# Two-part probabilities and values in a DSA attention tail, with engine orders written out as tables

## The chip, the cores and the metric

One core of a Trainium2 chip runs the kernel. Its engines are TensorE (PE in the rows, with its weight loads as PEld), VectorE (DVE), ScalarE (ACT), GpSimd (POOL) and SyncE (SP), which issues the loads. The metric is device time in microseconds for one call; lower is better.

## The reference

Two layers over x of 512 tokens and 1024 channels, each a mixer and a SwiGLU FFN (d_ff 2816), with a root-mean-square norm ahead of each.

The even layer's mixer has two halves. DSA attention: 8 query heads and 2 key/value heads of 64; an index score with 4 small heads picks for each query the best 128 keys; the softmax runs over these.

```
rel = relu(einsum(qi, k_idx)); score = einsum(rel, w) * IDX_SCALE   # causal
_, sel = lax.top_k(score, n_sel)                                    # n_sel = 128
p = softmax(q . k_sel * 64**-0.5);  o = p @ v_sel
```

A pooling half takes moving averages over 2, 4, 8 and 16 tokens, a 128x128 product for each group, and a scale. Both halves together go through `ev_w_out` (1024x1024).

The odd layer's mixer is stick-breaking attention with 16 heads of 64: `a = exp(log_sigmoid(z) - reversed cumsum of softplus(z))`, `o = a @ v`, then `od_w_out`. Each FFN is `(silu(h@w1) * (h@w3)) @ w2`.

## The kernel before

Activations are held transposed: channels on the partitions, the 512 tokens along a row, so x is eight tiles of 128x512 (`xs`). A weight or activation that needs more than one fp32r product is held as a rounded part and a rest, (h, l), and a dense product is three fp32r products: wh·ah, wh·al, wl·ah (`prods`, L202; lines L205 to L207). 

Each layer's attention is a list of small steps, `EVEN_ORDER` and `ODD_ORDER`. Every step is a function that issues its instructions; the program is traced in that order, and a scheduler with a model of the durations then decides the order on each engine, under the data dependences. Each engine runs its own list strictly in order, and waits for the others by semaphores. PSUM has eight banks of 128x512; `take` and `give` hand them out, and `EVEN_BANKS` (L47) says which step takes which banks.

Even layer, in the names of the steps: `qi`, `ki` are projections of the index heads, `st` and `sb` the norm's statistics and their broadcast, `q`, `kj` the projections of queries and keys, `z` the index scores (L750, L751, then ACT L753, DVE L757/L759, POOL L760), `sel` the choice of keys in blocks of 128 queries (MAX8 L770, MATCH_REPLACE8 L771, 16 rounds in a block, and the mask `bias[b]` at L773), `nat` (`step_nat`) makes v, 128 tokens on the partitions, in one tile for each key/value head j with zeros in the other head's half (L794). Then, for block b, head pair j and chunk k of 128 keys: `s` (`step_s`) computes four score tiles with the mask added as a third product (L874 to L876), takes a row maximum (DVE L879, POOL L880), the exponential (ACT L882), its reciprocal (DVE L888) and scales (L889: L177 on ACT or L181 on POOL). `pt` (`step_pt`) transposes four heads' probabilities into one of two 't' banks (L896), ACT copies them out (L898). `av` (`step_av`) multiplies them by v in F32 (`Bank.mm`, recorded at L225) into one bank 'o' for both j, 2(b+1) products, and at the last ACT writes oh (L911) and DVE ol (L912). Blocks 0 and 1 end before the last masks are there; blocks 2 and 3 are the last. `u`, `y`, `op` are the pooling half and its output products, `oa` the attention's output products; at each `oa` (and at each output step `x` of the odd layer) a chunk of x is complete, and `Norm.chunk` makes its parts hh and hl (L268, L269) and adds its squares on POOL into acc (L280).

The FFN begins with the first products of tiles that need no norm factor (`Plain`, `start`), with `nrm.stats()` behind 24 of them (PE L286, DVE L288, POOL L291); later tiles (`Job`) use sums of weights and of pairs of chunks (POOL L352 to L355 and L492 to L495). `bcast` (L293) spreads the factor over the partitions (PE L297); `follow` ties each of its products behind a product of the first Job.

Of the kernel before, what the change touches and what calls it, by code (L numbers as in the profile page):

```python
# [8 lines left out]
F32 = mybir.dt.float32  # L9
F32R = mybir.dt.float32r  # L10
# [6 lines left out]
P = 128  # L17
# [5 lines left out]
EPS = 1e-6  # L23
NSEL = 128

SPLIT = {'k1': ('pool', 'dve'),
 'ki': ('act', 'dve'),
 'nat_0': ('dve', 'dve'),
# [15 lines left out]
SPHI = {'A': 'act', 'B': 'pool', 'C': 'act'}  # L44
AHI = {'A': 'pool', 'B': 'act', 'C': 'act'}
KDUP = 'pool'
EVEN_BANKS = {'mm': (0, 1, 2), 's': (3, 4), 't': (5, 6), 'o': (7,), 'oa': (0, 1, 2, 3, 4, 5, 6, 7)}  # L47
ODD_BANKS = {'qk': (0,), 'A': (1,), 'B': (3,), 'C': (5,), 'o': (6,), 'v': (1, 2, 5, 6, 7), 'x': (0, 3, 4, 5), 'st': (4, 6), 'y': (7, 3, 4, 2, 1, 5, 0, 6)}
PRN = ('act', 'pool', 'act', 'pool')
WRAW = 3  # L50
# [54 lines left out]
]  # L105
NEG = -1e30
GONE = -3e38
GONE_TEST = -2.5e38
# [3 lines left out]
def f32(ap):  # L112
    return ap.bitcast(F32)
# [3 lines left out]
def tile_trunk(ctx, tc, x, gains, qk_gain, pool_scale, w_a, w_nat, pool_w, w_o0, w_qk, w_v, w_o1, w13, w2, out):  # L117
# [91 lines left out]
    def follow(m, first, why):  # L209

        tc.add_manual_dep(
            m.ins,
            first.ins.name,
            mybir.DependencyInfo(mybir.DependencyClass.NoSync, mybir.DependencyReason.DATA),
            reason=why,
        )
# [24 lines left out]
    class Norm:  # L241
# [48 lines left out]
            self.rcol = stat.tile([P, NB], F32, name=f"rcol{i}", tag="rcol")  # L290
            gp.tensor_tensor(self.rcol, ms, mhalf[:, 0:NB], op=ALU.pow)  # L291

        def bcast(self, banks=range(8), after=None):  # L293
            i = self.idx
            pb = take(banks)
            for b in range(NB):
                m = te.matmul(  # L297
                    pb[:, b * P : (b + 1) * P],
                    self.rcol[:, b : b + 1].to_broadcast([P, P]),
                    ident,  # L300
                    start=True,
                    stop=True,
                )
                if after is not None:
                    follow(m, after, "behind products that wait for less")
            self.rb = stat.tile([P, T], F32, name=f"rb{i}", tag="rb")
            ve.tensor_copy(self.rb, pb)
            give(pb)
# [93 lines left out]
    def ffn(stage):  # L402
# [220 lines left out]
        for f in range(1, NP):  # L623
            for w in range(2):
                x = Job(f, w)
                for who, p in ((x, 1), (x, 2), (y, 4), (x, 6), (y, 3), (x, 5), (x, 7)):
                    if who is not None:
                        m = who.prod(p)
                    elif p == 4:
                        nrm.bcast(after=m)  # L630
                        for d in start:
                            d.done()
                y = x
                q, r = divmod(f, 2)
                if q:
                    Down(q - 1, 2 * r + w)
# [13 lines left out]
    def even(nrm, nxt, w_first, after):  # L650
        with ExitStack() as es_wk:
# [22 lines left out]
            vs = [ap.tile([P, NB, P], F32, name=f"v{j}") for j in range(2)]  # L674
            for j in range(2):
                gp.memset(vs[j][:, :, OWN[1 - j]], 0.0)
            bias = {b: ap.tile([P, (b + 1) * P], BF16, name=f"bias{b}") for b in range(NB)}
            gp.memset(bias[0], 0.0)
            gp.affine_select(
# [96 lines left out]
            def step_nat():  # L776
# [14 lines left out]
                for b in range(NB):  # L791
                    ps = pns[b]
                    for j in range(2):
                        ac.activation(  # L794
                            vs[j][:, b, OWN[j]], ps[:, 64 * j : 64 * j + 64], AF.Copy, scale=nrm.rcol[:, b : b + 1]
                        )
                    for j in range(2):
                        ksq = wk.tile([P, 64], F32, name=f"ksq{b}_{j}", tag="ksq")
                        ac.activation(
                            ksq, ps[:, 128 + 64 * j : 192 + 64 * j], AF.Square, accum_out=kss[:, b, j : j + 1]  # L800
                        )
                    ac.copy(kn[:, b].rearrange("p a b -> p (a b)"), ps[:, 128:256])
                    give(ps)
# [89 lines left out]
            def step_pt(b, j, k):  # L893
                pt = take(EVEN_BANKS["t"])
                for c in range(4):
                    te.transpose(pt[:, c * P : (c + 1) * P], S["pr", b, j, c][:, k * P : (k + 1) * P], ident)  # L896
                pT = wk.tile([P, T], F32, name=f"pT{b}_{j}_{k}", tag="pT")
                ac.copy(pT, pt)  # L898
                give(pt)
                S["pT", b, j, k] = pT  # L900

            def step_av(b, j, k):
                if ("po", b) not in S:
                    S["po", b], S["bank", b], S["left", b] = take(EVEN_BANKS["o"]), Bank(), 2 * (b + 1)
                po = S["po", b]
                S["left", b] -= 1
                S["bank", b].mm(po, vs[j][:, k, :], S["pT", b, j, k], stop=(S["left", b] == 0))
                if S["left", b] == 0:
                    bs = slice(b * P, (b + 1) * P)
                    p3 = po.rearrange("p (a b) -> p a b", b=P)  # L910
                    ac.copy(oh[:, :, bs], p3)  # L911
                    ve.tensor_sub(ol[:, :, bs], p3, f32(oh[:, :, bs]))  # L912
                    give(po)
# [330 lines left out]
    ffns[1].run()  # L1244


# [1 line left out]
def _station(w):  # L1248

# [53 lines left out]
```

## Time and profile before

| | before |
|---|---|
| median of 3 runs | 1184.28 us (1182.9 to 1185.0) |
| the profiled execution | 1183.68 us |
| its span in the profile | 1181.9 us |
| PE busy | 1143.6 us (97%) |
| DVE busy | 862.1 us (73%) |
| ACT busy | 606.1 us (51%) |
| POOL busy | 547.9 us (46%) |

The span is what the profile covers, the rest of the 1183.68 lies around it. Busy time is the time that the engine's instructions cover; matmuls are pipelined, so a matmul's duration in a row is longer than the distance to the next. The granted clock is a share of TensorE's full 2.4 GHz; 0.5 is 1.2 GHz. "idle before <-releaser" says how long the engine stood still before an instruction and what ended it.

### The profile page before, as it was taken

The numbers are of one execution on the slowest core, as the hardware profiler recorded it, in microseconds if no ns is written. First come the engines' busy times: TensorE is split into PE (matmuls) and PEld (weight loads), VectorE is DVE, ScalarE is ACT, GpSimd is POOL, SyncE is SP. The second block draws the span as 40 slices with busy tenths as digits, with TensorE's granted clock in tenths as the row PEclk, the third lists the DMA queues.
The fourth block names the chain that finished last, engine by engine and source line by source line (L and its number), as shares of the span: only waits on it lengthen the run. The fifth ranks groups of instructions, "written<-read, shape, count | busy, mean of one in ns | idle before, by whom it ended". The sixth has DMA issues, their size and how long they took to land.

```text
span 1181.9 us, 17814 instructions
## 1 busy us (share of the span) xinstructions
PE 1143.6 (97%) x6854; PEld 1005.8 (85%) x6856; DVE 862.1 (73%) x1180; ACT 606.1 (51%) x929; POOL 547.9 (46%) x506
## 2 busy tenths in 40 slices
PE   7998989999999999999999999999799999999998
PEld 4885747799999999998888888888699999999997
DVE  7699936688778677757467778877678877676764
ACT  5354566454444444436257788866354444444441
POOL 4166646766444444403033345434876444454420
PEclk9999999899999999999999999999999999999999
DMA  5221112123333333323321111114122332333321
GB/s 202 74 87 59 54 36 95 48 90 108 108 107 93 102 105 94 108 73 97 106 94 45 52 36 54 54 54 127 34 90 87 111 109 96 100 108 108 108 90 71
DMA packets 37667, 102.60 MB, mean 87 GB/s; under 512 B 4560, under 2 KB 7120, under 8 KB 37584
## 3 DMA queue, kind: packets, MB, share of 16 engines
q1 hardware_dynamic: 37152, 101.47, 27.5%
q8 instruction: 53, 0.87, 0.3%
q14 instruction: 30, 0.25, 0.1%
q10 hardware_dynamic: 432, 0.02, 0.0%
HBM read 99.37 MB, written 2.10 MB: 86 GB/s over the span
## 4 chain that ended last, share of the span: by engine, by line
PE 73%; DVE 9%; POOL 8%; issue 5%; ACT 3%; DMA 1%; SPq 0%; POOLq 0%; DVEq 0%; ACTq 0%
PE psum L526 10%; PE psum L528 10%; PE psum L527 10%; PE psum L205 10%; PE psum L206 10%; PE psum L207 10%; PE psum L225 6%; DVE score L771 1%; DVE m L770 1%; PE psum L1027 1%; PE psum L1028 1%; PE psum L1029 1%; POOL acc L280 1%; POOL s L494 1%; POOL s L492 1%
## 5 line engine op out<-in xcount | busy, mean ns | idle before, releaser
L599 DVE TENSOR_TENSOR x<-x,psum 128x512 f32<-128x512 f32 x88 | 60.4, 686 | 119.6 <-PE psum L207 119.4
L492 POOL TENSOR_TENSOR s<-raw_w 128x512 f32<-128x512 f32 x40 | 60.2, 1505 | 178.8 <-DMA raw_w<-in_w_dram 154.1
L206 PE MATMUL psum<-gsl,wh_w 128*128 128x512 f32 x352 | 137.7, 391 | 0.0
L207 PE MATMUL psum<-gsh,wl_w 128*128 128x512 f32 x352 | 135.4, 390 | 0.0
L205 PE MATMUL psum<-gsh,wh_w 128*128 128x512 f32 x352 | 135.2, 391 | 0.0
L577 POOL TENSOR_TENSOR c<-c,rb 128x512 f32<-128x512 f32 x40 | 61.2, 1530 | 118.3 <-ACT c L576 118.3
L410 ACT CAST wh_w<-raw_w 128x1024 fp32r<-128x1024 f32 (+1 forms) x48 | 47.0, 980 | 114.5 <-PE psum L206 106.6
L526 PE MATMUL psum<-hh,wh_t 128*128 128x256 f32 x320 | 90.1, 282 | 0.5 <-DVE c L559 0.5
L526 PE MATMUL psum<-hh,wh_a 128*128 128x256 f32 x320 | 90.1, 282 | 0.5 <-ACT wh_a L410 0.5
L528 PE MATMUL psum<-hh,wl_s 128*128 128x256 f32 x320 | 90.3, 283 | 0.0
L526 PE MATMUL psum<-hh,wh_s 128*128 128x256 f32 x320 | 90.3, 283 | 0.0
L527 PE MATMUL psum<-hl,wh_t 128*128 128x256 f32 x320 | 90.3, 282 | 0.0
L527 PE MATMUL psum<-hl,wh_s 128*128 128x256 f32 x320 | 89.9, 281 | 0.0
L527 PE MATMUL psum<-hl,wh_a 128*128 128x256 f32 x320 | 89.8, 281 | 0.0
L528 PE MATMUL psum<-hh,wl_t 128*128 128x256 f32 x320 | 89.7, 280 | 0.0
L528 PE MATMUL psum<-hh,wl_a 128*128 128x256 f32 x320 | 89.6, 281 | 0.0
L410 ACT CAST wh_a<-raw_w 128x1024 fp32r<-128x1024 f32 x40 | 42.0, 1050 | 71.8 <-PE psum L206 57.4
L207 PEld LDWEIGHTS psum<-gsh,wl_w 128*128 128x128 f32 x352 | 66.2, 188 | 12.9
L206 PEld LDWEIGHTS psum<-gsl,wh_w 128*128 128x128 f32 x352 | 66.2, 188 | 12.1
L205 PEld LDWEIGHTS psum<-gsh,wh_w 128*128 128x128 f32 x352 | 65.8, 188 | 11.8
L411 DVE TENSOR_TENSOR wl_a<-raw_w,wh_a 128x1024 fp32r<-128x1024 f32 x40 | 65.8, 1646 | 12.9 <-ACT wh_a L410 12.9
L411 DVE TENSOR_TENSOR wl_w<-raw_w,wh_w 128x1024 fp32r<-128x1024 f32 (+1 forms) x48 | 64.6, 1346 | 3.6 <-ACT wh_w L410 3.5
(357 smaller groups left out, 3780.7 us busy)
## 6 DMA issues: line engine op xcount, KB each, us to landing
raw_w<-in_w_dram SPq DMA_DIRECT2D x88, 512.0 KB, 3.6
raw_w<-in_w_dram SPq DMA_DIRECT2D x80, 256.0 KB, 3.0
raw_v<-in_w_v_dram SPq DMA_DIRECT2D x8, 512.0 KB, 3.7
raw_q<-in_w_qk_dram SPq DMA_DIRECT2D x8, 512.0 KB, 3.6
raw_k<-in_w_qk_dram SPq DMA_DIRECT2D x8, 512.0 KB, 3.7
raw_o<-in_w_o_dram SPq DMA_DIRECT2D x8, 512.0 KB, 3.6
x<-in_x_dram SPq DMA_DIRECT2D x8, 256.0 KB, 4.7
raw_q<-in_w_a_dram SPq DMA_DIRECT2D x4, 512.0 KB, 4.8
```

The lines of the kernel that those rows point to most:

```text
L205: te.matmul(ps, wh, ah, start=(first and i == 0), stop=False)
L206: te.matmul(ps, wh, al, start=False, stop=False)
L207: te.matmul(ps, wl, ah, start=False, stop=(last and i == n - 1))
L225: m = te.matmul(dst, lhsT, rhs, start=self.first is None, stop=stop, skip_group_check=True)
L410: ac.copy(h[:, :n], src)
L411: ve.tensor_sub(l[:, :n], src, f32(h[:, :n]))
L492: gp.tensor_add(z[0], a21, a22)
L526: te.matmul(ps, wh, ah, start=first, stop=False, skip_group_check=True)
L527: te.matmul(ps, wh, al, start=False, stop=False, skip_group_check=True)
L528: m = te.matmul(ps, wl, ah, start=False, stop=(k == KC // 2 - 1), skip_group_check=True)
L577: gp.tensor_mul(d, d, nrm.rb)
L599: ve.tensor_add(xs[n], xs[n], self.ps[i])
```

## The change

- v gets a second pair of tiles, `vp[j]`: in head j's own half the rounded v, in the other half the rest v − rounded v. Eight small copies on ACT and eight subtractions on DVE in `step_nat`.
- In blocks 2 and 3 (`PACKED = 2`) the transposed probabilities are held as h (ACT, rounded) and l (DVE, the rest, out of PSUM); the 't' bank is given back behind both. `packed_av` multiplies `vp[j]` by h and by l, two fp32r products; the half of the bank on the other head's partitions holds the products with v's rest. Each j has a bank of its own, from banks 7 and 2, and ends with a copy of that half (cr, ACT), an add (DVE), and oh (ACT) and ol (DVE) for its 64 partitions.
- `bcast` no longer ties its products behind a Job's.
- `ENGINE_ORDER`: for each engine a list of its instructions' numbers in program order; at the end of the program each one listed is tied, without a semaphore, behind the one listed before it. PE's list has 3212 of its instructions (the whole even layer to the first Jobs of the first FFN, and the last products of that FFN over the odd layer into the last FFN), DVE's 690, ACT's 574, POOL's 355, SP's 110 loads. The rest of both FFNs isn't listed.

Decoded into steps, the lists say among other things: on PE `st` stands within `qi`, `sb` right behind `ki`, `z 1` behind 12 products of `q` (before: 48 of `q 0` and `q 1`); the products of `op` 3 to 7 lie between the scores of block 2 and those of block 3; behind the first score product of block 3 stand 24 score products, 48 transposes and 27 products with v, and then `oa`, in the order 4, 5, 1, 3, 2 for the products with oh, the rest behind; the FFN's statistics stand behind 96 products of oa, 70 of Plain and 22 of Job. On DVE the subtractions for l stand behind the last mask; ahead of it are the eight for v and two reductions of block 2 more than before. On POOL the first pair sum is that of chunks 0 and 1. In the odd layer single products of `q`, `k`, `v` and `x` alternate with the small ones of `z`, `s`, `o`; in the last FFN the statistics stand behind 78 Plain and the factor's broadcast further behind, with 24 Job products between, and POOL's power (L291) ahead of sums of weights. The loads on SP change places: pool_w 2 and 3 earlier, the first of oa ahead of pool_w 1.

```diff
+PACKED = 2
-EVEN_BANKS = {'mm': (0, 1, 2), 's': (3, 4), 't': (5, 6), 'o': (7,), 'oa': (0, 1, 2, 3, 4, 5, 6, 7)}
+EVEN_BANKS = {'mm': (0, 1, 2), 's': (3, 4), 't': (5, 6), 'o': (7,), 'o2': (7, 2), 'oa': (0, 1, 2, 3, 4, 5, 6, 7)}
...
+ENGINE_ORDER = {
+    "PE": (
+        "0-21 24-25 22-23 48-49 26-40 50 41-42 72 43-47 51-56 73-75 57-71 76-78 188-189 79 190-198 80-83 199 "
...
+    "DVE": (
+        "0 15 1 16-18 14 3 19 4 2 5-13 22 38 25 39 20-21 40 26 23 28-29 24 49-50 27 30-36 64-65 55 37 56 "
...
-        def bcast(self, banks=range(8), after=None):
+        def bcast(self, banks=range(8)):
...
-                m = te.matmul(
+                te.matmul(
...
-                if after is not None:
-                    follow(m, after, "behind products that wait for less")
...
-                        nrm.bcast(after=m)
+                        nrm.bcast()
...
+            vp = [ap.tile([P, NB, P], F32R, name=f"vp{j}") for j in range(2)]
...
                     for j in range(2):
+                        v = vs[j][:, b, OWN[j]]
+                        ac.copy(vp[j][:, b, OWN[j]], v)
+                        ve.tensor_sub(vp[j][:, b, OWN[1 - j]], v, f32(vp[j][:, b, OWN[j]]))
...
+                if b >= PACKED:
+                    h = wk.tile([P, T], F32R, name=f"ph{b}_{j}_{k}", tag="pT")
+                    l = wk.tile([P, T], F32R, name=f"pl{b}_{j}_{k}", tag="pl")
+                    ac.copy(h, pt)
+                    ve.tensor_sub(l, pt, f32(h))
+                    give(pt)
+                    S["pT", b, j, k] = h, l
+                    return
...
+            def packed_av(b, j, k):
+                if ("po", b, j) not in S:
+                    S["po", b, j], S["bank", b, j], S["left", b, j] = take(EVEN_BANKS["o2"]), Bank(), b + 1
+                po = S["po", b, j]
+                S["left", b, j] -= 1
+                h, l = S["pT", b, j, k]
+                S["bank", b, j].mm(po, vp[j][:, k, :], h)
+                S["bank", b, j].mm(po, vp[j][:, k, :], l, stop=(S["left", b, j] == 0))
+                if S["left", b, j]:
+                    return
+                bs = slice(b * P, (b + 1) * P)
+                cr = wk.tile([P, T], F32, name=f"cr{b}_{j}", tag="rl")
+                ac.copy(cr[OWN[j], :], po[OWN[1 - j], :])
+                of = wk.tile([P, T], F32, name=f"of{b}_{j}", tag="rl")
+                ve.tensor_add(of[OWN[j], :], po[OWN[j], :], cr[OWN[j], :])
+                give(po)
+                o3 = of[OWN[j], :].rearrange("p (a b) -> p a b", b=P)
+                ac.copy(oh[OWN[j], :, bs], o3)
+                ve.tensor_sub(ol[OWN[j], :, bs], o3, f32(oh[OWN[j], :, bs]))
...
+    traced = [m for m in nc.cur_bb.bb.instructions]
+    for engine, runs in ENGINE_ORDER.items():
...
+        for a, b in zip(places, places[1:]):
+            tc.add_manual_dep(
+                own[b],
+                own[a].name,
+                mybir.DependencyInfo(mybir.DependencyClass.NoSync, mybir.DependencyReason.DATA),
+                reason="order of the engine",
+            )
```

## Rows read from the trace of the kernel before

**Rows 1.** The page, busy time: us, share of the span, instructions.

```profile
PE 1143.6 (97%) x6854; PEld 1005.8 (85%) x6856; DVE 862.1 (73%) x1180; ACT 606.1 (51%) x929; POOL 547.9 (46%) x506
```

**Rows 2.** Windows by stage: length, busy time of each engine, granted clock, DMA share, GB/s.

```profile
31.30:148.40 117.10, 110.42 (x573) 88.45 (x573) 104.11 (x265) 54.90 (x136) 65.72 (x83) 1.00 0.22 65
148.40:180.60 32.20, 28.07 (x116) 14.79 (x116) 10.01 (x26) 20.79 (x46) 12.31 (x24) 1.00 0.10 33
...
600.00:810.00 210.00, 204.56 (x1086) 178.05 (x1085) 159.15 (x175) 154.42 (x203) 82.76 (x101) 0.99 0.18 54
810.00:890.00 80.00, 72.85 (x425) 63.99 (x423) 62.37 (x67) 44.82 (x65) 58.89 (x40) 0.96 0.27 85
```

**Rows 3.** Windows of DVE alone, in the even layer.

```profile
52.30:146.00 93.70, 91.17 (x244) 1.00 0.21 64
146.00:180.60 34.60, 10.21 (x28) 1.00 0.09 32
```

**Rows 4.** Timeline of DVE, the last mask.

```profile
145.61 0.43 DVE L773 TENSOR_SCALAR bias<-score 128x512 bf16<-128x512 f32 x1
```

**Rows 5.** Timeline of PE: start, us, line, tiles; idle time before and its releaser.

```profile
46.16 0.74 PE L750 MATMUL psum<-kih,qi 128*128 128x256 f32 x4
...
130.12 0.39 PE L206 MATMUL psum<-yl,wh_op 128*128 128x512 f32 x1
130.35 1.02 PE L225 MATMUL psum<-pT,v 128*128 128x512 f32 x2
131.21 0.38 PE L896 MATMUL psum<-ident,pr 128*128 128x128 f32 x2
131.42 0.60 PE L225 MATMUL psum<-pT,v 128*128 128x512 f32 x1
...
180.59 0.73 PE L205 MATMUL psum<-oh,wh_oa 128*128 128x512 f32 x2 [0.68 <-ACT oh L911]
...
221.59 1.43 PE L286 MATMUL psum<-ones,acc 128*128 128x1 f32 x8 [1.99 <-POOL acc L280]
...
840.52 0.50 PE L206 MATMUL psum<-hl,wh 128*128 128x512 f32 x1 [2.50 <-DVE hl L346]
...
843.08 0.62 PE L206 MATMUL psum<-hl,wh 128*128 128x512 f32 x1 [1.12 <-DVE hl L346]
...
856.87 1.37 PE L297 MATMUL psum<-ident,rcol 128*128 128x128 f32 x5 [2.44 <-POOL rcol L291]
```

**Rows 6.** Windows of PE alone: length, busy time, granted clock, DMA share, GB/s.

```profile
222.90:229.00 6.10, 6.10 (x16) 0.51 0.00 0
...
841.00:847.50 6.50, 5.38 (x17) 0.74 0.00 0
854.00:861.00 7.00, 4.56 (x26) 0.76 0.08 13
```

**Rows 7.** Instructions of DVE, 60 to 181: busy us, mean ns; idle before.

```profile
L879 DVE TENSOR_REDUCE mx<-psum 128x1 f32<-128x512 f32 x8 | 5.5, 690 | 3.8 <-PE psum L896 1.4 <-PE psum L876 1.2 <-POOL mx L880 1.0
...
L912 DVE TENSOR_TENSOR ol<-psum,oh 128x512 fp32r<-128x512 f32 x4 | 2.7, 687 | 7.8 <-ACT oh L911 7.7
...
L856 DVE TENSOR_TENSOR rq<-psum,r 128x8 f32<-128x8 f32 x4 | 0.6, 159 | 0.1
```

**Rows 8.** Instructions of ACT, 60 to 181: busy us, mean ns; idle before.

```profile
L898 ACT COPY pT<-psum 128x512 f32<-128x512 f32 x20 | 11.1, 587 | 8.5 <-PE psum L896 8.5
```

**Rows 9.** Timeline of POOL, first pair sum and last add into acc.

```profile
187.00 0.74 POOL L352 TENSOR_TENSOR b<-b 128x256 f32<-128x256 f32 x1 [12.92 <-PE psum L206]
...
218.67 2.86 POOL L280 TENSOR_TENSOR acc<-acc,sq 128x512 f32<-128x512 f32 x2
```

**Rows 10.** Waits of PE, 600 to 810: us in total, times, longest.

```profile
PE psum L225 <- DVE slB L1139: 3.8, 5, 1.1
```

**Rows 11.** Waits of PE, 148.4 to 180.7: us in total, times, longest.

```profile
PE psum L225 <- ACT pT L898: 1.8, 3, 0.6
```

More of the change, by code (lines that the diff above doesn't have):

```diff
@@ L105 @@
 ]
+ENGINE_ORDER = {
[88 rows of a table added]
+    ),
+    "DVE": (
[25 rows of a table added]
+    ),
+    "Activation": (
[21 rows of a table added]
+    ),
+    "Pool": (
[12 rows of a table added]
+    ),
+    "SP": (
+        "9-18 23-25 33-34 26-32 35-36 39-42 37 55 38 56-58 60-61 59 65 62 66-68 70 69 71-72 74 73 75-78 "
+        "168-190 200-204 206 205 211 207-208 212-214 216 215 217-218 220 219 221-224 227-228 225-226 229-230 "
+        "232 231 233-236"
+    ),
+}
 NEG = -1e30
@@ L797, in step_nat @@
                     for j in range(2):
+                        v = vs[j][:, b, OWN[j]]
+                        ac.copy(vp[j][:, b, OWN[j]], v)
+                        ve.tensor_sub(vp[j][:, b, OWN[1 - j]], v, f32(vp[j][:, b, OWN[j]]))
+                    for j in range(2):
                         ksq = wk.tile([P, 64], F32, name=f"ksq{b}_{j}", tag="ksq")
@@ L900, in step_pt @@
                 S["pT", b, j, k] = pT
+            def packed_av(b, j, k):
[17 more added lines that the diff above has]
+                ve.tensor_sub(ol[OWN[j], :, bs], o3, f32(oh[OWN[j], :, bs]))
             def step_av(b, j, k):
+                if b >= PACKED:
+                    return packed_av(b, j, k)
                 if ("po", b) not in S:
@@ L1244, in tile_trunk @@
     ffns[1].run()
+    traced = [m for m in nc.cur_bb.bb.instructions]
+    for engine, runs in ENGINE_ORDER.items():
+        own = [m for m in traced if m.engine == getattr(mybir.EngineType, engine)]
+        places = []
+        for run in runs.split():
+            first, _, last = run.partition("-")
+            places += range(int(first), int(last or first) + 1)
+        for a, b in zip(places, places[1:]):
[5 more added lines that the diff above has]
+            )
 def _station(w):
```

143 rows, old and new, of the table ENGINE_ORDER are left out of this document.

## The prediction

> **What bounds the kernel now.** First the busy shares: PE is busy for 1143.6 of 1181.9 us [rows 1], so any large gain has to come out of PE's own work, out of its 38 us without work, or out of products that run at the lower clock. The windows by stage [rows 2] say where these lie. In 31.3 to 148.4 PE is busy for 110.42 of 117.10 us, in 148.4 to 180.6 (the end of the even layer's attention) for 28.07 of 32.20, in 600 to 810 (the odd layer) for 204.56 of 210, and in 810 to 890 (odd layer into the last FFN) for 72.85 of 80, at a mean clock of 0.96. The FFNs between are full. The change touches just these stages.
>
> Next the row of DVE in the even layer [rows 3]. In 52.3 to 146.0 it is busy for 91.17 of 93.7 us: that is the chain of MAX8 and MATCH_REPLACE8 that selects keys, and its last product, the mask of block 3, starts at 145.61 [rows 4]. After that DVE has 24.4 of 34.6 us free. All scores of block 3 need that mask, so the even layer is limited by DVE up to 146, then by a tail on PE with some waiting. The selection itself begins when the index scores do (z 1 at 46.16 on PE [rows 5]), and those stand behind 48 products of q 0 and q 1 which it does not need.
>
> The timeline of PE [rows 5] gives the prices. One fp32r product of 512 columns starts 0.23 us before the next (130.12 to 130.35), though the row shows longer. One F32 product of the probabilities, shown as two records, takes 131.21 − 130.35 = 0.86 us. The same view shows the long stops at the hand-overs: 0.68 us before the first oa product, 1.99 before the statistics of the first FFN's norm, and 2.50, 1.12 and 2.44 around the last FFN's norm. After such stops the clock falls to half: 0.51 over 222.9 to 229.0, 0.74 and 0.76 in the two later windows [rows 6].
>
> **The change, part by part.**
>
> *Products of blocks 2 and 3.* Block 2 has 6 and block 3 has 8 F32 products; they become 28 fp32r products. 14 × 0.86 = 12.04 us go, 28 × 0.23 = 6.4 come: −5.6 us of PE, if PE sets the pace there. If waiting does, it is 0. I take it whole, since 28.07 of the last 32.20 us are busy; it is a part of the next sum and not added to it.
>
> *What is added for it.* DVE gets 14 subtractions out of PSUM (as the 687 ns of L912 [rows 7]: 9.6 us), eight small ones for v, and at the four ends an add and a subtraction in place of two L912 (+6 × 0.69 = 4.1). For v's parts of 64 columns the nearest row is the one of 8 columns, 159 ns (L856), and 687 ns for 512 is the upper end; near the lower, 0.2 each, 1.6 us. ACT gets eight small copies, and 8 for 2 at the ends (+6 × 0.59 = 3.5 us [rows 8]). In the table only the eight v parts and two more reductions of block 2 (L879, 690 ns) stand ahead of the last mask on DVE, 1.6 + 1.4 = 3 us; the rest, 13.7 − 1.4 us, stands behind it, where 24.4 us are free. Without that cover it would be 12 us longer.
>
> *Order of the even layer.* The table puts z 1 behind 12 products of q instead of 48: 36 × 0.23 = 8.3 us earlier. The selection takes as long as now plus 3 us, so the last mask comes at about 146.0 − 8.3 + 3 = 140.7. The products of op 3 to 7 are placed before the scores of block 3, so PE has work until then. What is left behind the mask in the table are 24 score products, 48 transposes and 27 products with v: (24 + 27) × 0.23 + 48 × 0.107 = 16.9 us (0.107: the two transposes from 131.21 to the next product at 131.42 [rows 5]). The waits there were 4.1 us (32.20 − 28.07); with fewer products as cover and a longer path (copy, subtraction, product; then cr, add, oh at the end, 3 × 0.6 to 0.69 where one oh copy stood) I take 12. oa begins at 140.7 + 16.9 + 12 = 169.6: −11. The lower bound: PE's busy time of both windows, 110.42 + 28.07 − 5.6 = 132.9, without a stop from 31.3 on, gives 164.2, or −16.4. The upper bound is the rival on the banks below, +6.
>
> *Hand-over to the first FFN.* Stop 1.99 us, and 6.10 us at 0.51, which lose 3.0: at most −5. The table does oa 4, 5, 1, 3, 2 with their first products early, so the pair sums on POOL, which began 6.4 us behind oa's start (187.00 [rows 9] against 180.59), begin some 14 us behind it. Against that it places the statistics behind all 70 Plain and 22 Job products (with 96 of oa, 41 us). POOL's adds stand closer in its table. Between −5 and +7.6 (the whole late start) I take −2.
>
> *Odd layer.* No work changes. The waits are 210 − 204.56 = 5.4 us, 3.8 of them products on slB [rows 10]; the table puts projections of the next heads between. Bounds −5.4, all filled, and +5.4, as much waiting again where the fixed order doesn't fit; I take −3, since the fill is the same stock of products, spread finer.
>
> *Hand-over to the last FFN.* Stops 2.50 + 1.12 + 2.44 = 6.1 us, and lost clock of 5.38 × 0.26 + 4.56 × 0.24 = 2.5: 8.6. The bcast is no longer tied behind a Job product, and rcol is put ahead of POOL's weight sums. Bounds 0 and −8.6; I take −6, since for all three stops the table moves the late work forward.
>
> *The rest.* The loads on SP change places only among themselves, hidden by queues that are ahead (no PE stop there names a DMA in these windows). Unlisted instructions, most of both FFNs, keep their order: 0.
>
> Sum: −11 − 2 − 3 − 6 = −22 us. From the profiled execution, 1183.68, that is 1161.7; the median of the runs shown is 0.6 above it, so 1162.3, and I forecast 1162.
>
> **The rivals.**
>
> *Arithmetic alone.* The tables only move stalls about: a fixed order made on expected durations meets others on the chip, and each engine waits in order. Then −5.6 is left: 1178. For it: four orders are pinned over some 600 us. Against: the stops named are long and have a named late instruction, and the table moves those.
>
> *Everything filled.* −16.4 − 5 − 5.4 − 8.6 = −35: 1149. Against it, the tail has hardly any filler left.
>
> *Late POOL.* The first pair sum comes 14 us behind oa's start instead of 6.4, and the statistics wait 7.6 us longer, with the same slow products behind: −22 + 2 + 7.6 = −12, 1171. It decides from the point where POOL's chain, 34.5 us now (187.00 to 221.5), is not shortened by more than those 7.6 us.
>
> *The two t banks, slower.* A bank is given back only after the subtraction: 0.43 + 0.59 + 0.69 = 1.71 us, where it was 1.02. Two banks give a transposed tile each 0.86 us instead of 0.51. If that sets the pace, the saved PE time shows as waiting, 14 × 0.35 = +4.8, and the end has 1.27 us more: +6, and if the hand-overs gain nothing either, 1190. It decides where PE has under 0.86 us between two transposes; by the table there are 0.43 + 0.46 and a share of the scores, 0.46, so 1.35 us, and only for the last four tiles 0.89. The wait on pT now is 1.8 us in all [rows 11].
>
> *DVE sets the end.* It is full to 146 [rows 3]; if the added 13.7 + 1.6 = 15.3 us all lengthen it, 1199. The row behind 146 speaks against that: 24.4 us are free. The Trainium skill (Perfetto Trace Analysis, "Identifying the Most-Contended Engine") says that VectorE's occupancy is a fair measure of its limit and to relieve the engine with the highest occupancy first; by that rule, an edit that loads DVE in this layer should cost and not gain. The trace agrees for 52.3 to 146 (97%) and not for the tail (30%).
>
> *No effect.* The scheduler's order was as good: 1184.
>
> **How the numbers follow.** Forecast 0.56, arithmetic alone 0.14, late POOL 0.08, everything filled 0.08, t banks 0.06, DVE 0.03, no effect 0.05. Under 0.2% (2.4 us) a measurement of this kernel can't tell from no change. Faster: 0.86; within 0.2%: 0.05; slower: 0.09. For 8 in 10 the range takes in everything filled, with its bounds, and arithmetic alone: 1146 to 1179.
>
> **What would show it.** z 1 on PE near 38 instead of 46.2; the last mask near 141; oa near 170; no stop over 1 us before the statistics; the rows of 840 to 857 (some 20 us earlier) without stops over 1 us and at full clock; waits on slB under 2 us. Wrong would be a transpose that waits for pl, a first pair sum 14 us behind oa with PE standing at the statistics, or DVE busy without gaps between the last mask and oa.

## The result and the profile after

The changed kernel takes 1200.45 us (median of 4 runs, 1199.35 to 1200.74) against 1183.59 before: 1.0143 times, 95% interval 1.0127 to 1.0159. The forecast was 1162, so 22 us faster; it is 17 us slower instead. The page of the changed kernel, busy time:

```profile
span 1197.8 us, 17858 instructions
PE 1151.2 (96%) x6856; PEld 1003.8 (84%) x6856; DVE 888.5 (74%) x1208; ACT 613.2 (51%) x943; POOL 557.0 (47%) x506
```

By the prediction's prices PE has 5.6 us less to do, yet it is busy for 7.6 us more [rows 1]: its rows grow longer where the granted clock is lower, as the windows around the first hand-over show further down. Its timeline at the places of [rows 5] (index scores, oa, start of the first FFN, start of the last FFN):

```profile
36.96 0.34 PE L913 MATMUL psum<-kih,qi 128*128 128x256 f32 x1
...
182.74 0.79 PE L368 MATMUL psum<-oh,wh_oa 128*128 128x512 f32 x1 [2.04 <-ACT oh L1095]
219.31 0.36 PE L687 MATMUL psum<-hh,wh_a 128*128 128x256 f32 x1 [1.92 <-DVE x L359]
220.83 0.79 PE L370 MATMUL psum<-hh,wl 128*128 128x512 f32 x1 [0.81 <-DVE wl L572]
232.54 0.38 PE L449 MATMUL psum<-ones,acc 128*128 128x1 f32 x2 [0.62 <-POOL acc L443]
...
836.67 0.50 PE L369 MATMUL psum<-hl,wh 128*128 128x512 f32 x1 [1.15 <-DVE hl L507]
845.84 0.39 PE L687 MATMUL psum<-hh,wh_a 128*128 128x256 f32 x1 [1.54 <-ACT wh_a L571]
854.45 0.38 PE L688 MATMUL psum<-hl,wh_a 128*128 128x256 f32 x1 [2.66 <-DVE hl L507]
868.33 1.16 PE L460 MATMUL psum<-ident,rcol 128*128 128x128 f32 x8 [1.30 <-POOL rcol L454]
881.04 0.39 PE L689 MATMUL psum<-hh,wl_a 128*128 128x256 f32 x1 [1.19 <-DVE wl_a L572]
```

The index scores come 9.2 us earlier, yet oa begins 2.2 us later (182.74 against 180.59), the statistics of the first FFN 11.0 later (232.54 against 221.59). Stops at the last FFN are still there, in part others than before. To follow the shift further, one row of ScalarE deep in the first FFN, before at 293.04 with the same wait of 1.91:

```profile
302.71 0.37 ACT L695 COPY u<-psum 128x256 f32<-128x256 f32 x1 [1.91 <-PE psum L689]
```

So it is 9.7 us behind there. In the odd layer nothing is added: the kernels have the same number of PE instructions left at 793.5 and 803.1, so the changed one is 9.6 us behind. At 960 and 976 the same holds with a shift of 16.0, so the rest arises at the last hand-over; the spans differ by 15.9.

| | forecast | measured |
|---|---|---|
| even layer, start of oa | −11 | +2.2 |
| hand-over to the first FFN | −2 | +7.5 |
| odd layer | −3 | about 0 |
| hand-over to the last FFN | −6 | +6.2 |

VectorE in the even layer: the first round of the selection and the last mask (timeline), then the windows from the same start to the end of the mask and on to oa, which answer to [rows 3, 4]. A line of windows gives the stretch, its length, VectorE's busy time (instructions), the granted clock, DMA share and GB/s.

```profile
45.07 0.43 DVE L933 MAX8 m<-score 128x8 f32<-128x256 f32 x1
...
153.04 0.95 DVE L936 TENSOR_SCALAR bias<-score 128x512 bf16<-128x512 f32 x1
```

```profile
31.30:153.99 122.69, 112.06 (x273) 0.99 0.20 59
153.99:182.74 28.75, 21.30 (x44) 1.00 0.15 52
```

The selection begins at 45.07, before at 52.37, but lasts 108.9 us instead of 93.7. The mask is complete at 153.99, not at 140.7. From there to oa it is 28.75 us; the forecast had 28.9. The two stretches up to the mask, split at the first round of the selection, in the kernel before and in the changed one:

```profile
31.30:52.37 21.07, 12.73 (x21) 1.00 0.26 78
52.37:146.04 93.67, 91.21 (x244) 1.00 0.21 64
31.30:45.07 13.77, 9.94 (x16) 1.00 0.20 55
45.07:153.99 108.92, 102.12 (x258) 0.98 0.20 59
```

### The profile page after: what moved, and what is told of

It reads as the page before. It is cut to its first block, busy times and chain, and to the rows that moved or that the text cites. A ratio compares the mean times of both kernels' runs of the same rounds, so it can differ in the third digit from the quotient of the medians.

```text
span 1197.8 us, 17858 instructions
## 1 busy us (share of the span) xinstructions
PE 1151.2 (96%) x6856; PEld 1003.8 (84%) x6856; DVE 888.5 (74%) x1208; ACT 613.2 (51%) x943; POOL 557.0 (47%) x506
## 4 chain that ended last, share of the span: by engine, by line
PE 65%; POOL 8%; DVE 5%; issue 4%; ACT 2%; DMA 0%; POOLq 0%; DVEq 0%; ACTq 0%
PE psum L687 10%; PE psum L689 10%; PE psum L688 10%; PE psum L370 9%; PE psum L368 9%; PE psum L369 9%; PE psum L388 5%; POOL acc L443 2%; PE psum L1225 1%; PE psum L1227 1%; POOL eB L1296 1%; PE psum L1226 1%; POOL shB L344 1%; DVE gsl L598 1%; POOL b L513 1%
## 5 line engine op out<-in xcount | busy, mean ns | idle before, releaser
L738 POOL TENSOR_TENSOR c<-c,rb 128x512 f32<-128x512 f32 x40 | 64.4, 1611 | 110.6 <-ACT c L737 110.6
```

The lines of the kernel that those rows point to most:

```text
L738: gp.tensor_mul(d, d, nrm.rb)
```

## The experiments

In the kernel before, VectorE's window from 31.3 to the end of the mask is this; in three other kernels of the table further down its busy time is nearly the same.

```profile
31.30:146.04 114.74, 103.94 (x264) 1.00 0.22 66
```

### The parts without the orders, and the orders without the parts

```diff
-ENGINE_ORDER = { ... }
+ENGINE_ORDER = {}
```

> The two-part products without any engine order (the scheduler sets all orders); the broadcast is not tied, as in the changed kernel. Theory, the written orders cost the time: -6 to +1 us against the kernel before (14 products of 0.86 us become 28 of 0.23), 1178 to 1185. Rival, the parts cost it (14 more subtractions out of PSUM on VectorE, two t banks held longer): +8 to +16 us, 1192 to 1200.

1189.87 us, 1.0046 (1.0029 to 1.0063 times the kernel before): 5 us slower, between the two theories. The mask starts at 150.78 and oa at 187.00.

```profile
31.30:151.91 120.61, 108.36 (x273) 0.94 0.20 59
151.91:187.00 35.09, 22.68 (x46) 1.00 0.14 46
```

All the delay is there before the mask; behind it the tail (from the complete mask to oa) is 35.1 us, as before (34.6), though PE should have 5.6 us less to do in it. So nothing of that term shows here.

The opposite, F32 products of before with all lists (a list skips the instructions that the F32 products don't have):

```diff
-PACKED = 2
+PACKED = 4
...
+        places = [p for p in places if own[p] is not None]
```

> The engine orders with the F32 products of before: the instructions that only the two-part products have are left out of the lists, all others stand in the same order; the broadcast is not tied. Theory, the orders cost: +14 to +22 us, 1198 to 1206. Rival, the parts cost: -8 to +4 us, 1176 to 1188, since VectorE has 15 us less to do in the even layer.

1202.83 us, 1.0152 (1.0135 to 1.0169). The orders alone cost as much as the whole change. The mask starts at 153.63 and oa at 183.97, both as in the changed kernel, and without any of the parts' work on VectorE:

```profile
31.30:154.58 123.28, 111.59 (x266) 0.99 0.20 60
154.58:184.00 29.42, 8.55 (x24) 1.00 0.15 52
```

The tail's 29.4 us, too, come from the order and not from the parts. A likely reason stands in the group of block 2's row maxima: 7 of 8 are ahead of the mask in the changed kernel, 4 before, so fewer score tiles are left behind it. Below, in the kernel with early scores only it is two, and the tail 43.4 us; with VectorE's list left out none, and 48.4. The changed kernel's rows up to the mask:

```profile
L1046 DVE TENSOR_REDUCE mx<-psum 128x1 f32<-128x384 f32 x7 | 3.8, 549 | 0.9 <-PE psum L1043 0.8
L963 DVE TENSOR_TENSOR vp<-v,vp 128x64 fp32r<-128x64 f32 x8 | 1.7, 223 | 0.0
```

### Each layer's lists

```diff
+        places = [p for p in places if p < FIRST_ODD[engine]]
```

> The changed kernel with the orders of the even layer and the start of the first FFN alone; everything behind is left to the scheduler. The shift of 9 us that the trace of the changed kernel has in the first FFN stays in either theory; the theory that each order costs at its own place: +7 to +11 us, 1191 to 1195. Rival, an order spoils what comes behind it or the parts cost it all: as the changed kernel, +15 to +18.

1192.76, 1.0065 (1.0050 to 1.0080): +8 us, as the theory said. With the other half (`p >`):

> The changed kernel with the orders of the odd layer and of both its borders alone; the even layer is left to the scheduler. Theory, each order costs at its own place: +6.7 us from the hand-over to the last FFN, and the two-part products free: +1 to +8 us, 1185 to 1192. Rival, the parts cost: +12 to +18, 1196 to 1202.

1198.33, 1.0112 (1.0097 to 1.0127): +13.5, in the rival's range. Against the parts alone, run with it on the same chip, the lists of the odd layer and its borders cost 8.5 us; the theory counted the parts as free, which they aren't.

The lists cut at both hand-overs, so that attention's output products, the norms and both starts of an FFN are left to the scheduler:

```diff
+        places = places[: TAIL[engine][0]] + [p for p in places if TAIL[engine][1] <= p < TAIL[engine][2]]
```

> The changed kernel with its lists cut at both hand-overs to an FFN: the even layer up to its last product with v, and from the last products of the first FFN up to the odd layer's second round of output products; the output products of attention, the norm and the FFN's start are left to the scheduler. Theory, the lists cost 7 us at the first hand-over and 7 at the last, and 2 us inside the even layer: +2 to +4 us against the kernel before, 1186 to 1188. Rival, the even layer's list leaves its successors in a bad state whoever orders them: +10 or more.

1188.96, 1.0038 (1.0024 to 1.0052): +5.9, between the two but well away from the whole lists' 17. The first pair sum on GpSimd begins 8 us behind oa (183.32), 17 in the changed kernel:

```profile
191.31 1.24 POOL L514 TENSOR_TENSOR b<-b 128x256 f32<-128x256 f32 x1 [15.28 <-ACT b L507]
```

So some 11 of the 17 us (17 less 5.9) are the written orders around the hand-overs. The count of PE instructions that are left divides it further: each kernel is compared with the one before at the same count, and the shift is taken from oa's start to the first FFN (first hand-over), from there to 793 us, and from there to 970.

| lists tied there | first hand-over | odd layer | last hand-over |
|---|---|---|---|
| changed kernel | +7.5 | −0.1 | +6.4 |
| all other kernels with them | +5.6 to +11.6 | −0.1 to +3.0 | +6.1 to +6.5 |
| layers alone (cut at the hand-overs) | +1.2 | 0.0 | +1.6 |
| none, with the two parts | +1.0 to +1.6 | −1.5 to 0.0 | −0.4 to +0.9 |
| none, F32 products | −0.4 to −0.1 | −1.7 to 0.0 | +0.2 to +0.3 |

So the odd layer's list neither helps nor hurts within the layer (3.0 stands in the lists alone, the eight others with it have 0.3 at most), its end at the last FFN costs over 4 us, and of the first hand-over's 7.5 us the two parts have some 1.5 and the lists the rest.

### Is the early selection worth anything?

PE's beginning alone is tied (to the first index scores), with F32 products:

```diff
+TAIL = {"PE": slice(0, 114)}
...
+        places = places[TAIL[engine]] if engine in TAIL else []
```

> F32 products as before; of all lists only PE's beginning is tied, up to the first index scores, which stand ahead of most products of q as in the changed kernel. The step of the prediction: the selection begins 7 to 9 us earlier and so does the last mask, 137 to 139, oa with it: -5 to -8 us, 1176 to 1179. Theory now, VectorE's other work of that time only moves in between the selection's rounds, and the mask comes when VectorE has done it all: mask 143 to 147, time -3 to +2, 1180 to 1186.

1189.13, 1.0051 (1.0030 to 1.0071). The selection begins at 45.30, 7.1 us earlier, and the mask starts at 144.11, only 1.5 earlier. That is the new theory's mask; its time was missed by 3 us, because oa comes at 187.93, 43.4 us behind the mask: what had been done before the mask (two of block 2's row maxima among it) is now done behind it.

```profile
31.30:144.54 113.24, 103.80 (x259) 0.95 0.20 60
```

VectorE has been busy for 103.8 us when the mask is there, 103.9 in the kernel before. Next, the changed kernel without VectorE's own list in that part:

```diff
+        if engine == "DVE":
+            places = [p for p in places if p > 500]
```

> The changed kernel, with VectorE's own list left out up to the first FFN; all other lists are tied. Theory, VectorE's written order holds the selection up: mask 3 to 8 us earlier than 154, oa below 179, 1192 to 1197. Rival, the work that the other engines' lists hand to VectorE ahead of the mask does it, whatever its own order: mask 151 to 155, 1198 to 1202.

1215.26, 1.0265 (1.0235 to 1.0294). Half of the theory holds: the mask starts at 144.91, 8 us earlier than in the changed kernel, after 104.2 us of VectorE's work. The other half falls: oa begins at 193.69. The other engines' lists are as they were, and PE waits for what VectorE now does later, as in these rows:

```profile
98.33 0.47 PE L368 MATMUL psum<-hh,wh_u 128*128 128x512 f32 x1 [1.58 <-DVE mixed L1144]
...
125.52 0.50 PE L369 MATMUL psum<-yl,wh_op 128*128 128x512 f32 x1 [1.99 <-DVE yl L1153]
```

### Where the parts' 5 us come from

The parts without lists, v's eight subtractions on GpSimd:

```diff
-                        ve.tensor_sub(vp[j][:, b, OWN[1 - j]], v, f32(vp[j][:, b, OWN[j]]))
+                        gp.tensor_sub(vp[j][:, b, OWN[1 - j]], v, f32(vp[j][:, b, OWN[j]]))
```

> The two-part products without lists, with v's eight small subtractions on GpSimd in place of VectorE. Theory, the parts cost 5 us by what VectorE has to do ahead of the last mask: mask 1.5 to 4 us earlier than 151.9, 1185 to 1188. Rival, they cost it by the t banks behind the mask: as the parts alone, 1189 to 1191.

1185.14, 1.0005 (0.9989 to 1.0020): the 5 us are gone. The eight subtractions took VectorE only 1.5 us with the parts alone; the rest of the 4.4 us between 108.36 and 103.94 is mostly in other instructions, which took longer there (see the even layer below). VectorE's window is that of the kernel before to the last digit of its busy time, and the mask starts at 146.23:

```profile
31.30:146.66 115.36, 103.94 (x264) 1.00 0.21 67
146.66:180.99 34.33, 22.80 (x47) 1.00 0.08 31
```

Behind the mask VectorE does 12.6 us more than in the kernel before (22.80 against 10.2 [rows 3]), and oa begins 0.4 us later. So the parts cost and save the same there, in sum. PE's own busy time in the tail falls from 30.4 to 27.5 us, and its waits take that up: 1.9 us for the subtractions' l, which the kernel before doesn't have (us in total, times, longest),

```profile
PE psum L229 <- DVE pl L909: 1.9, 6, 0.7
```

and 2.0 in front of oa where it was 0.7. The same with two parts in block 3 alone:

> The same with two parts in block 3 alone, so that none of the new VectorE work stands ahead of the mask: 8 products of 0.86 us become 16 of 0.23, 3.2 us less on PE behind the mask. Theory: mask at 146 to 147, time -3 to 0, 1180 to 1184. Rival, the banks behind the mask cost: +2 to +5.

With `PACKED = 3`: 1185.95 us, 1.0020 (1.0008 to 1.0033); mask at 145.90, oa at 181.07. The mask is as expected, the 3 us are not gained.

### What sets the tail?

Of the four lists only the places from block 3's scores to the last product with v are tied, with F32 products:

```diff
+TAIL = {"PE": slice(618, 726), "DVE": slice(256, 300), "Activation": slice(142, 181), "Pool": slice(125, 141)}
```

> F32 products as before, and only the list of the tail (block 3's scores to the last product with v) tied. Theory, the tail's 5 to 6 us come from its order and not from the two parts, and the mask stays at 146: -3 to -6 us, 1178 to 1181. Rival, the tail is short only because the whole list has spent PE's other work before the mask: -1 to +1.

1188.23, 1.0033 (1.0018 to 1.0048). Mask at 145.92, oa at 185.16: neither 1178 nor no change. The tail's order by itself makes the tail 4 us longer; it was short only with the whole lists, which put more ahead of the mask. The same with the two parts:

> Two-part products with only the tail's list. Theory: the mask comes 6 us late as in the run of the parts alone, the tail is 6 us shorter: 0, 1183 to 1186. Rival, as the parts alone: +5, 1188 to 1191.

1195.89, 1.0095 (1.0076 to 1.0115), mask at 150.17, oa at 191.51: the mask is as late as the theory had it, but the tail is 40.2 us, 5 longer than with the parts alone and not 6 shorter. Both theories missed.

A third bank for block 3's score tiles, on the kernel before:

```diff
+EVEN_BANKS = {'s3': (3, 4, 2), 'op': (0, 1), ...
-                ps = take(EVEN_BANKS["s"])
+                ps = take(EVEN_BANKS["s"] if b < 3 else EVEN_BANKS["s3"])
...
-                ps = take(EVEN_BANKS["mm"])
+                ps = take(EVEN_BANKS["mm"] if n < 5 else EVEN_BANKS["op"])
```

> The kernel before, with a third bank (2) for the score tiles of block 3; the output products 5 to 7 of the pooling half use banks 0 and 1. Theory, the tail behind the mask is a chain through two score banks (12 tiles of some 1.65 us: product, maximum, exponential) and not PE's work: tail 31 to 33 us in place of 34.6, time -2 to -4, 1180 to 1182. Rival, ScalarE or the transposes set it: -1 to +1.

1183.01, 0.9993 (0.9983 to 1.0002). The tail falls by 2.2 us, from 34.6 to 32.3, as expected, but the mask comes 1.8 later; the time is the rival's.

```profile
147.28 0.52 DVE L773 TENSOR_SCALAR bias<-score 128x512 bf16<-128x512 f32 x1
```

And a third bank together with the two parts:

> The two-part products without lists, v's subtractions on GpSimd, and bank 1 as the third bank of block 3's scores; the output products 5 to 7 have bank 0 alone. Theory, PE's saved 5.6 us can show once the chain is shorter: tail 28 to 32 us, time -3 to -6, 1178 to 1181. Rival, the end of each head pair (copy, add, copy) and VectorE's subtractions take its place: -1 to +2.

1186.66, 1.0024 (1.0011 to 1.0037), mask at 146.45, oa at 182.25: the theory falls, the tail stays long (35.4 us). In front of oa stand 2.04 us for copy, add and copy where it was 0.68, and PE waits 1.9 us for l. Against the third bank alone the tail is 3 us longer (the banks of the output products differ as well).

### The first hand-over

In VectorE's list an add into x5 stands behind a rest of pair sums (hl) that waits for ScalarE's hh, and this for GpSimd's last pair sums (timeline of the changed kernel):

```profile
211.36 0.96 DVE L507 TENSOR_TENSOR hl<-b,hh 128x512 fp32r<-128x512 f32 x1 [0.50 <-ACT b L506]
215.56 1.05 ACT L518 CAST hh<-b 128x1024 fp32r<-128x1024 f32 x1 [3.63 <-POOL b L515]
216.65 1.91 DVE L519 TENSOR_TENSOR hl<-b,hh 128x1024 fp32r<-128x1024 f32 x1 [4.32 <-ACT hh L518]
218.48 0.68 DVE L359 TENSOR_TENSOR x<-x,psum 128x512 f32<-128x512 f32 x1
```

PE's last output product of attention ended at 214.6; the add waited until 218.48, and PE's stop at 219.31 names it. The edit moves it ahead:

```diff
-319 312 321 313 309 314 318 329 320
+319 312 321 313 314 318 309 329 320
```

> The changed kernel; in VectorE's list the add into x5 and a weight rest stand ahead of a rest of pair sums (hl of chunks 2 and 3) that waited 4.3 us for POOL at the head of VectorE's queue. Theory, this waiting head held the add, the bank and so PE (1.92 and 0.81 us, then products at half the clock): -3 to -5 us against the changed kernel, 1195 to 1198. Rival, the statistics wait for POOL's late adds anyway: -1 to +1 against it, 1199 to 1202.

1201.35, 1.0146 (1.0127 to 1.0166): no gain. That stop is gone, and another has come; ScalarE's hh stands in its list behind squares that waited 1.92 and 0.99 us for GpSimd's acc:

```profile
227.61 0.38 PE L687 MATMUL psum<-hh,wh_a 128*128 128x256 f32 x1 [3.89 <-ACT hh L505]
```

Then PE's list and the other engines' lists, each alone carried on through the hand-over, on top of the lists cut there:

```diff
-TAIL = {"PE": (726, 3122, 4366), ...
+TAIL = {"PE": (1170, 3122, 4366), ...
```

> The run with the layers' lists alone, with PE's list carried on through the first hand-over (output products of attention, start of the first FFN); the other engines are free there. That run is 3 us behind the kernel before in the middle of the first FFN, the changed kernel 9. Theory, PE's order (products of chunks 4 and 5 first, the first pair sum of chunks 0 and 1 17 us after the start) costs the 6 us: 8 to 10 us behind there, time 1193 to 1196. Rival, the other engines' fixed orders cost it, each with an instruction that waits at its head: 2 to 5 us behind, 1187 to 1191.

1196.64, 1.0108 (1.0093 to 1.0123).

That is just past the theory's range. For the other engines, in the same way:

```diff
-... "DVE": (300, ...), "Activation": (181, ...), "Pool": (141, ...)
+... "DVE": (367, ...), "Activation": (247, ...), "Pool": (182, ...)
```

> The counterpart: lists of VectorE, ScalarE and GpSimd carried on through the first hand-over, PE free there. Theory, PE's order costs: 2 to 5 us behind in the first FFN, 1187 to 1191. Rival: 8 to 10 us behind, 1193 to 1196.

1197.17, 1.0116 (1.0099 to 1.0133), just past the rival's range. Either kind of list costs as much as both: 7.7 and 8.2 us over the lists cut there; by the count of PE's instructions this hand-over takes 8.9 and 7.8 us, 7.5 with all lists. So the two don't divide the cost, and the pair as it was posed has no winner. In both the first pair sum begins at 200.4 to 200.9, 16.5 to 17.8 us behind oa. Last, that sum moved forward within the lists (output tiles 0 to 3 first on PE, and the same on VectorE, ScalarE and GpSimd); cut here to VectorE's adds into x and to GpSimd:

```diff
-... 310-311 305 307 300 302 301 ...
+... 310-311 300 302 305 307 301 ...
...
-... 135 137 157 142-145 150-151 ...
+... 135 137 142-145 157 150-151 ...
```

> The changed kernel; in its lists attention's output products of tiles 0 to 3 stand first and in that order (then the others as they stood), the adds into x0 and x1 ahead of x2 and x3, ScalarE's parts of chunks 0 and 1 ahead of 2 and 3, and GpSimd's weight rest behind the first pair sums. Theory, the late first pair sum (17 us behind the start of these products, 6 before) costs most of the 7 to 9 us of this hand-over: first pair sum 7 to 10 us behind, -3 to -6 us against the changed kernel, 1194 to 1197. Rival, any fixed order costs here, wherever the pair sums begin: -1 to +2 against it, 1199 to 1202.

1198.70, 1.0131 (1.0112 to 1.0149). The first pair sum is 6.3 us behind oa, as in the kernel before, and the statistics come 2.0 us earlier than in the changed kernel:

```profile
188.95 0.74 POOL L512 TENSOR_TENSOR b<-b 128x256 f32<-128x256 f32 x1 [13.57 <-PE psum L369]
```

```profile
229.43 0.50 PE L368 MATMUL psum<-hl,wh 128*128 128x512 f32 x1 [1.20 <-DVE hl L506]
230.55 0.27 PE L448 MATMUL psum<-ones,acc 128*128 128x1 f32 x1 [0.62 <-POOL acc L442]
```

By the trace the late pair sum has a share of 2 us; the total can't tell that from nothing. The rest stays, with stops of 0.3 to 1.2 us.

### The untied broadcast

```diff
-                        nrm.bcast(after=m)
+                        nrm.bcast()
```

> The kernel before, with the broadcast of an FFN's norm no longer tied behind a Job's product: the third part of the change alone. All theories: -1 to +1 us, 1183 to 1185; more than 2 us slower would give this part a share of its own in the 16.

1184.06, 1.0006 (0.9996 to 1.0016): no share in it. No version here beats the kernel before.

## Why the prediction was wrong

**The even layer (−11 forecast, +2.2).** The step that failed is "The selection takes as long as now plus 3 us, so the last mask comes at about 146.0 − 8.3 + 3 = 140.7". What stands ahead of it held (index scores 9.2 us earlier), and so did the 28.9 us from the mask to oa (28.75), in part by luck: they count on PE's 5.6 us, which measured nothing, and the lists alone have 29.4 without them. But the selection took 15.2 us longer, not 3, since it is no chain of its own that can be moved. VectorE has it and other work to do in one stretch, and in the kernel before it is busy for 97% of the time from the selection's first round to the mask:

| kernel | VectorE busy from 31.3 to the mask | mask complete | oa |
|---|---|---|---|
| before | 103.9 | 146.0 | 180.6 |
| early scores only | 103.8 | 144.5 | 187.9 |
| changed, VectorE's list left out | 104.2 | 145.3 | 193.7 |
| parts alone, v's rests on GpSimd | 103.9 | 146.7 | 181.0 |
| parts alone | 108.4 | 151.9 | 187.0 |
| lists alone | 111.6 | 154.6 | 184.0 |
| changed | 112.1 | 154.0 | 182.7 |

In each of these VectorE is busy for 90 to 92% of the stretch, and the mask is there when it has done what stands ahead of it. The 15.2 us are 10.9 of work and 4.3 of idle time. Of the work, 2.8 us stood ahead of the selection before: the earlier start only lets them in between. An estimate from the rows by shape divides the 8.1 us that are left: added instructions have 3.1 (eight for v's rests 1.8, three reductions 1.7, less some small ones), so the forecast's 3 us was right in size; some 4.0 are the same instructions taking longer, and the last 1 is that they overlap less. In the lists alone the two are 2.0 and 4.0, in the parts alone 1.9 and 3.8. So most of the delay is no work that was added or moved; the last section shows what the longer instructions have in common. In the two kernels with an early start and 104 us it is less work (1.6 and 2.7 us) and longer instructions (2.3 and 2.6), so their equal sums are not the same work, and what was taken out ahead of the mask came behind it, where PE waited for it.

The Trainium skill (Perfetto Trace Analysis, "Identifying the Most-Contended Engine") says that VectorE's occupancy is a fair measure of how near it is to its limit, and to optimize the engine with the highest occupancy first. The traces agree up to the mask: eight subtractions off VectorE, with the order that came of it, were worth 5 us there, and 5.6 us off PE nothing.

**PE's 5.6 us.** "I take it whole, since 28.07 of the last 32.20 us are busy": wrong, in sum it measured 0. With the parts and the mask where it was, the tail is 34.3 us against 34.6: PE is busy for 2.9 us less and waits 2.7 us more, 1.9 us in all for l. What does set the tail was only narrowed down: a third score bank shortens it by 2.2 us in the kernel before, and the two parts need 2.04 us in place of 0.68 at its end.

**The first hand-over (−2 forecast, +7.5).** "POOL's adds stand closer in its table. Between −5 and +7.6 (the whole late start) I take −2" failed: the result is at the upper bound. The first pair sum begins 17.4 us behind oa's start (at 200.10), where 14 was read from the table. But the rival "late POOL", which would have given this number, is not what the runs show in the main: it expected PE to stand at the statistics, and PE stood there 0.62 us. Moving the sum forward gave back 2 us. From oa's start to the row of ScalarE in the first FFN both kernels execute 670 matmuls (PE before, then changed, and the slowest stretch of the changed one):

```profile
180.59:293.04 112.45, 110.46 (x670) 0.97 0.28 86
182.74:302.71 119.97, 114.28 (x670) 0.94 0.26 81
222.00:226.00 4.00, 4.00 (x14) 0.50 0.68 233
```

So of the 7.5 us 3.7 are stops (2.0 in all before, 5.7 now, the longest 1.92) and 3.8 longer products; the granted clock, 0.94 instead of 0.97, would give about that much, an estimate (119.97 × 0.06 − 112.45 × 0.03). The longest stands behind an instruction that waited at the head of VectorE's list; the others weren't followed up. Lists on PE alone or on the others alone are enough for it; moving one instruction moved the stop elsewhere. With the lists cut there 1.2 us are left, as with the parts alone. Whether another fixed order would do better isn't shown.

**The odd layer (−3, about 0).** Products waited 3.8 us for slB [rows 10]; among PE's waits of the same stretch, the smallest of which is 0.3 us, slB no longer stands, and its time without work falls from 5.4 to 2.6 us, as forecast:

```profile
600.00:812.00 212.00, 209.44 (x1101) 1.00 0.19 55
```

By the count of PE's instructions nothing came of it: PE is busy for as much more. Why is open.

**The hand-over to the last FFN (−6, +6.2).** The step that failed is "for all three stops the table moves the late work forward": one of the three is nearly gone, two stand at the same kind of place (hl 1.15 for 1.12, rcol 1.30 for 2.44), and three others came (1.54, 2.66, 1.19 us), as at the first. By the count of PE's instructions this hand-over takes 6.1 to 6.5 us in all six kernels with the lists through it, 1.6 to 2.0 in the three with the lists cut there, and −0.4 to 0.9 without lists, so it is the lists' end that costs. PE before and in the changed kernel, between equal counts:

```profile
793.50:960.00 166.50, 159.35 (x994) 0.98 0.30 91
803.10:976.00 172.90, 161.83 (x995) 0.99 0.28 86
```

It stands for 11.1 us in place of 7.2, and its products take 2.5 us longer. The instruction there was not sought by an experiment.

**Rivals.** "Arithmetic alone" named the mechanism at the hand-overs ("a fixed order made on expected durations meets others on the chip, and each engine waits in order") but gave it no price, so it ended on the wrong side. "The two t banks" was right that the saved PE time would show as waiting, and wrong that 6 us would be added. "DVE sets the end" had the right engine and the wrong stretch: not the tail, where it had room (21.30 of 28.75 us), but what stands ahead of the mask; it was given 0.03. That its 1199 is near the measured 1200 is luck, since 13.7 of the 15.9 us arise behind oa's start.

## What to carry to other kernels

When an engine is full up to a deadline, add up everything it must finish by then, in the new order too, and with the durations that its instructions have beside their new neighbours on the other engines; an earlier start of the chain that ends there is worth no more than the idle time in front of it (8.3 us here, of which at most 1.5 came out). An order written out for every engine lets each late instruction hold up all that stand behind it, so price it by the waits at the heads of the lists and not by the stops of the old trace that it removes. PE at 87% in a stretch is no proof that less PE work makes it shorter; look for what releases its products.

## What the runs showed of the hardware beside that

The same VectorE instruction of 128x512, the last mask, took 0.43 us in the kernel before, 0.95 in the changed one and 1.13 with the parts alone; four scalings of 128x8 took 247 ns each before and 554 in the changed one. The traces show what goes with it: a GpSimd instruction that was running when it began. The changed kernel, then the parts alone:

```profile
152.33 0.68 DVE L934 MATCH_REPLACE8 score<-m,score 128x512 f32<-128x512 f32 x1
152.39 1.31 POOL L363 TENSOR_TENSOR x<-x,xa_op 128x512 f32<-128x512 f32 x1
153.04 0.95 DVE L936 TENSOR_SCALAR bias<-score 128x512 bf16<-128x512 f32 x1
```

```profile
150.58 1.05 POOL L185 TENSOR_SCALAR wh_oa<-raw_oa 128x1024 fp32r<-128x1024 f32 x1 [1.02 <-PE psum L210]
150.78 1.13 DVE L777 TENSOR_SCALAR bias<-score 128x512 bf16<-128x512 f32 x1
```

In all twelve kernels here in which the mask took over 0.43 us (0.52 to 1.13), a GpSimd instruction was running when it began, and the mask ended 0.27 to 0.29 us behind that one's end. In the other eight none was, and it took 0.41 to 0.43. Not every VectorE instruction does so: the MATCH_REPLACE8 beside the same GpSimd instruction kept its 0.68. In the changed kernel the longest scalings of 128x8 (0.89 and 0.98 us) and two subtractions of weights (2.09 and 1.77 us, 1.37 on average before) also began beside one, and ended 0.03 and 1.1 us behind its end. So these durations hold a wait for GpSimd, and an order decides how many such meetings there are. No run moved a GpSimd instruction for this alone.

After the stop of 2.04 us in front of oa the changed kernel's PE ran at 0.53 for 3.5 us, and the kernel with the outputs in order, with the same stop there, at 1.00. So a stop of that length alone doesn't decide it.

```profile
182.70:186.20 3.50, 3.46 (x9) 0.53 0.10 8
```

```profile
182.70:186.20 3.50, 3.28 (x13) 1.00 0.09 14
```
